# Twelve more chunks per layer as pairs of half products, in one stage ahead of the attention

## The chip, the cores and the metric

The kernel runs on one core of a Trainium2 chip. The metric is the time of one execution on the device in microseconds (us), as the median of several runs. The engines that matter here are PE (matrix products), DVE (vector operations), ACT (scalar engine, activations and copies), POOL (a fourth engine, here mostly an issuer of transfers) and SP (which only issues transfers). Each engine takes its instructions in a fixed order and waits at one until what it needs is there; everything behind it on that engine waits too.

## The reference, cut to what matters

Two layers are applied to 640 tokens (512 of a prompt, 128 of samples). In each, one wide projection `x @ w_in` is cut into parts that feed a gated MLP branch (A), a recurrent branch (B), a latent attention (C), an attention over a memory (M) and the gates that merge them:

```python
(a_u, a_v, a_g, b_x, b_g, c_q, c_kv, c_kr, c_g, m_q, gate_logits) = split_cols(x @ w_in)
oa, v_rows = gmlp_branch(a_u, a_v, ...)       # gelu(a_u) * (mix of layer_norm(gelu(a_v)))
oa = oa * silu(a_g)
ob = rglru_branch(b_x, ...) * silu(b_g)
oc = mla_branch(c_q, c_kv, c_kr, ...) * silu(c_g)
om = mem_attend(m_q, mem_k, mem_v)
g = sigmoid(gate_logits)                       # four gates of 1024 channels
merged = g[:, :, 0] * (oa @ w_a) + g[:, :, 1] * (ob @ w_b) + g[:, :, 2] * (oc @ w_c) + g[:, :, 3] * (om @ w_m)
x = layer_norm(ALPHA * x + merged @ w_out)
```

The change concerns how the parts `a_u` (512 channels, gelu), `c_g` and `b_g` (512 channels each, silu) are computed.

## The kernel before

All matrix products are done in fp32 by parts: each operand is split into a high and a low part (`split`: ACT casts the high part, DVE subtracts it to get the low one), and three products are added: high by high, low by high, high by low.

**Chunks.** A chunk is 128 channels of the projection. `fm_chunk` loads its 1024 x 128 weights (`wraw`, one transfer of 512 KB on SP's queue into one of three `raw` buffers), splits them (`whl`, into one of two `wh` and two `wl` buffers) and issues 48 matmuls of 128 x 320 into an accumulator of two PSUM banks: 8 blocks of the inner dimension, 3 parts, 2 halves of the tokens. An evacuation with gelu or silu follows (`gelu_u`, `silu_into`).

**Pairs of half products.** `fm_pair` computes two chunks at once by a scheme in the manner of Strassen: seven products of half the inner dimension, of 12 matmuls each, in place of eight. It needs four sums of quarters of the operand x (`xt` 1 to 4, made by `x_sums`, written to DRAM as `xsum` and read back by `x_sums_back`), and sums of the weights of the two chunks (`wsum`, on DVE). DVE then adds the products from PSUM (`psum`). Before the change only the merge gates are done so: 14 pairs per layer (the other four chunks of the gates go through `fm_chunk`).

**Order within a layer.** The latent projections c, the projection v (120 matmuls, then gelu on ACT), the latent transposes (`cqT_ps` and others), in layer 0 the memory's keys and values (`mem_kv`), the layer norm of v on DVE, two gelu chunks, the query product `q_ps`, the other gelu chunks, the token mixing (`mix`, which needs the weights `wmx` by way of POOL), the rest of the queries, four silu chunks of C each followed by one quarter of `x_sums`, keys and values, then the attention, into whose gaps a scheduler puts the remaining chunks, and the merge: pairs of gate chunks (`fp`) alternating with the branch products (`y`, 48 matmuls per pair of channels chunks, 24 in the last branch), then the output projection.

Instructions are put on each engine in an order that the scheduler of the framework works out; buffers and PSUM banks are reused in turn. A tile is waited for as a whole: two banks of one accumulator tile count as one thing in this.

Of the kernel before, what the change touches and what calls it, by code (L numbers as in the profile page):

```python
# [19 lines left out]
T = NP_ + NS  # L20
# [16 lines left out]
PRE_U = 2  # L37
# [3 lines left out]
def encoder_step(  # L41
# [141 lines left out]
    xsum = dr.tile([4, 128, 4, 2, TH], F32, name="xsum")  # L183

    for l in range(L):
# [105 lines left out]
        def x_sums(k, xh=xh, xl=xl):  # L291
            x0, x1 = tmp([128, T], "x0"), tmp([128, T], "x1")
            for i, x_ in enumerate((x0, x1)):
                DVE.tensor_tensor(
                    out=x_, in0=xh[i][:, k, :].bitcast(F32), in1=xl[i][:, k, :].bitcast(F32), op=ALU.add
                )
            t12 = tmp([128, T], "t12")
            t1, t2 = t12[:, lo_], t12[:, hi_]
            DVE.tensor_tensor(out=t1, in0=x0[:, lo_], in1=x0[:, hi_], op=ALU.subtract)
            DVE.tensor_tensor(out=t2, in0=t1, in1=x1[:, hi_], op=ALU.add)  # L300
            DVE.tensor_tensor(out=x0[:, hi_], in0=x0[:, hi_], in1=x1[:, hi_], op=ALU.subtract)
            DVE.tensor_tensor(out=x1[:, lo_], in0=x1[:, lo_], in1=t2, op=ALU.subtract)
# [12 lines left out]

        def fm_pair(c, take):
# [8 lines left out]
            ab, cd = acc("fp"), acc("fp")  # L325
            ba, bb, bc, bd = (o[:, j, 0:TH] for o in (ab, cd) for j in range(2))
# [16 lines left out]
            p1, u = t_[:, lo_], t_[:, hi_]  # L343
            wsum(ws[:, b_], r0[:, a_], r1[:, a_])
            wsum(r1[:, a_], r1[:, a_], r1[:, b_])
            wsum(ws[:, a_], r0[:, a_], r1[:, a_])
# [10 lines left out]
            wsum(r0[:, b_], r0[:, b_], ws[:, a_])  # L357
            w1 = whl(r1)
            product(ba, w1, 0, 1, True, False)
# [6 lines left out]
            psum(z0[:, hi_], ba, u, ALU.add)  # L366
            take(0, slice(0, T), z0)
            return z0, z1

# [872 lines left out]
```

## Time and profile before

| what | value |
|---|---|
| median of 3 runs | 1425.04 us (1424.37 to 1427.62) |
| profiled execution: its own time | 1428.68 us |
| its span, first to last instruction | 1427.0 us |
| PE busy | 1391.2 us, 97% of the span |
| DVE busy | 963.4 us, 68% |
| ACT busy | 596.9 us, 42% |
| POOL busy | 119.6 us, 8% |
| mean granted TensorE clock | 0.993 of full speed |

Busy time counts the instructions that compute; PE's matmuls overlap and are counted as one stretch. The profiled execution took 3.64 us more than the median.

### The profile page before, as it was taken

The page shows a single profiled execution, that of the slowest core. Times are in us where ns is not written, and L with a number is a line of the kernel's source. Part 1 is how long each engine was busy: PE and PEld are TensorE (multiplying, and loading weights), DVE is VectorE, ACT ScalarE, POOL GpSimd, SP SyncE. Part 2 cuts the span into 40 slices and gives each one's busy share as a digit, 9 for nine tenths or more (in the row PEclk, how much of TensorE's full clock was granted, in tenths as well). Part 3 has the DMA queues.
Part 4 walks back from the last instruction along what each step waited for, and adds up shares of the span by engine and source line. Part 5 has one row for each costly group of instructions (what it writes and reads, how often), then busy time and mean ns, then how long its engine had stood idle before and what let it go on. Part 6 is the DMA issues. An engine that isn't in the chain of part 4 may idle for free.

```text
span 1427.0 us, 22738 instructions
## 1 busy us (share of the span) xinstructions
PE 1391.2 (97%) x9040; PEld 1281.2 (90%) x9040; DVE 963.4 (68%) x1684; ACT 596.9 (42%) x1019; POOL 119.6 (8%) x248
## 2 busy tenths in 40 slices
PE   8999999999989999999999999999999999999997
PEld 8899987879989999998898999878799899999986
DVE  5664768566577777786844748585766577877866
ACT  5533444355534343444234335353655343334430
POOL 2011110012110000000111102001111000000000
PEclk9999999999999999999999999999999999999999
DMA  7443521523253333227353325126132423322343
GB/s 252 142 137 104 170 82 48 184 91 122 77 165 95 92 93 99 74 89 228 131 181 101 117 92 200 41 73 217 33 126 87 159 95 96 93 84 75 103 156 111
DMA packets 57529, 168.23 MB, mean 118 GB/s; under 512 B 6608, under 2 KB 15728, under 8 KB 55376
## 3 DMA queue, kind: packets, MB, share of 16 engines
q1 hardware_dynamic: 48880, 127.54, 28.7%
q0 software_dynamic: 8544, 39.25, 7.6%
q8 instruction: 71, 1.16, 0.3%
q14 instruction: 34, 0.28, 0.1%
HBM read 140.63 MB, written 24.82 MB: 116 GB/s over the span
## 4 chain that ended last, share of the span: by engine, by line
PE 82%; DVE 9%; DMA 4%; issue 2%; ACT 2%; POOL 0%; DVEq 0%; SPq 0%; ACTq 0%; POOLq 0%
PE fm L122 21%; PE fp L334 19%; PE y L122 12%; PE y_ps L1087 8%; PE v L137 4%; PE c L137 3%; PE sc_ps L693 3%; DMA raw<-in_w_fm 2%; PE pv_ps L717 2%; PE mem L137 2%; DVE wl L148 1%; PE pt_ps L710 1%; PE q_ps L122 1%; DMA mcache<-in_mem_kv 1%; DVE z L340 1%
## 5 line engine op out<-in xcount | busy, mean ns | idle before, releaser
L147 ACT CAST wh<-raw 128x1024 fp32r<-128x1024 f32 (+3 forms) x203 | 191.5, 943 | 367.4 <-PE fp L334 159.3
L148 DVE TENSOR_TENSOR wl<-raw,wh 128x1024 fp32r<-128x1024 f32 (+3 forms) x203 | 222.5, 1097 | 143.1 <-issue 56.1
L122 PE MATMUL fm<-xl,wh 128*128 128x320 f32 x832 | 200.9, 316 | 0.0
L122 PE MATMUL fm<-xh,wh 128*128 128x320 f32 x832 | 200.4, 317 | 0.4 <-DVE oc L527 0.4
L334 PE MATMUL fp<-xt,wh 128*128 128x320 f32 x896 | 149.9, 310 | 6.5 <-ACT wh L147 3.9
L122 PE MATMUL y<-bhl,wh 128*128 128x320 f32 x896 | 147.4, 316 | 2.3 <-DVE macc L969 1.0
L122 PEld LDWEIGHTS fm<-xh,wh 128*128 128x128 f32 x832 | 139.5, 188 | 7.5 <-issue 4.5
L122 PEld LDWEIGHTS fm<-xl,wh 128*128 128x128 f32 x832 | 140.3, 188 | 5.7 <-issue 5.2
L334 PEld LDWEIGHTS fp<-xt,wh 128*128 128x128 f32 x896 | 135.4, 188 | 8.7 <-ACT wh L147 5.5
L122 PE MATMUL fm<-xh,wl 128*128 128x320 f32 x832 | 142.8, 316 | 0.0
L122 PEld LDWEIGHTS y<-bhl,wh 128*128 128x128 f32 x896 | 137.6, 192 | 4.1 <-ACT wh L147 2.1
L122 PEld LDWEIGHTS fm<-xh,wl 128*128 128x128 f32 x832 | 125.8, 189 | 4.4 <-issue 3.3
L334 PE MATMUL fp<-xh,wh 128*128 128x320 f32 x336 | 100.4, 310 | 4.2 <-DVE z L340 2.1
L334 PE MATMUL fp<-xl,wh 128*128 128x320 f32 x336 | 100.4, 310 | 0.0
L334 PE MATMUL fp<-xt,wl 128*128 128x320 f32 x448 | 83.2, 309 | 0.0
L122 PE MATMUL y<-bhl,wl 128*128 128x320 f32 x448 | 76.3, 310 | 0.0
L334 PEld LDWEIGHTS fp<-xt,wl 128*128 128x128 f32 x448 | 70.1, 188 | 0.0
L122 PEld LDWEIGHTS y<-bhl,wl 128*128 128x128 f32 x448 | 68.6, 189 | 0.0
L334 PEld LDWEIGHTS fp<-xh,wh 128*128 128x128 f32 x336 | 63.3, 188 | 4.7 <-issue 4.7
L334 PE MATMUL fp<-xh,wl 128*128 128x320 f32 x336 | 64.0, 313 | 0.0
L334 PEld LDWEIGHTS fp<-xl,wh 128*128 128x128 f32 x336 | 63.4, 189 | 0.0
L340 DVE TENSOR_TENSOR z<-fp,tu 128x320 f32<-128x320 f32 x84 | 40.9, 486 | 31.8 <-PE fp L334 31.7
(326 smaller groups left out, 2317.8 us busy)
## 6 DMA issues: line engine op xcount, KB each, us to landing
raw<-in_w_fm SPq DMA_DIRECT2D x108, 512.0 KB, 3.7
xsum<-xs POOLq DMA_DIRECT2D x32, 320.0 KB, 2.9
xt<-xsum POOLq DMA_DIRECT2D x8, 1280.0 KB, 6.2
raw<-in_w_br SPq DMA_DIRECT2D x20, 512.0 KB, 3.9
mcache<-in_mem_kv SPq DMA_DIRECT2D x8, 1024.0 KB, 5.1
raw<-in_w_out SPq DMA_DIRECT2D x16, 512.0 KB, 4.5
osrc<-oscr POOLq DMA_DIRECT2D x20, 320.0 KB, 3.8
raw<-in_w_v SPq DMA_DIRECT2D x8, 512.0 KB, 3.8
```

The lines of the kernel that those rows point to most:

```text
L122: PE.matmul(out=out[:, j, 0:TH], lhsT=a(k), rhs=b(k)[:, j * TH:(j + 1) * TH], start=(n == 0), stop=(n == len(steps) - 1),)
L137: PE.matmul(out=o[:, 0:width], lhsT=a(ci * nk_per + j)[:, t * 128:(t + 1) * 128], rhs=w[:, j * width:(j + 1) * width], start=(ci == 0 and ...
L147: ACT.copy(out=dst_h, in_=src)
L148: DVE.tensor_tensor(out=dst_l, in0=src, in1=dst_h.bitcast(F32), op=ALU.subtract)
L334: PE.matmul(out=o, lhsT=a[:, k0:k0 + 128], rhs=b[:, k, :], start=(first and n == 0), stop=(n == len(steps) - 1), skip_group_check=True,)
L340: DVE.tensor_tensor(out=out, in0=x, in1=y, op=op)
L693: PE.matmul(out=s[:, 0:nk], lhsT=qT[0:kr_, h, ts_], rhs=kT[h // 4][0:kr_, h % 4, 0:nk], start=True, stop=True,)
L710: PE.transpose(tps[:, k * 128:(k + 1) * 128], p[:, k * 128:(k + 1) * 128], ident)
L717: mm = PE.matmul(out=ops[64 * e:64 * e + 64, hp * 128:(hp + 1) * 128], lhsT=vc[:, k, h * 64:(h + 1) * 64], rhs=pt[:, k * 128:(k + 1) * 128 ...
L1087: PE.matmul(out=o[j], lhsT=mg[k // 2][:, a, k % 2, t * 128:(t + 1) * 128], rhs=wo[k, w][:, j * 512:(j + 1) * 512], start=(k == 0 and p == ...
```

## The change

Twelve chunks per layer (four of `a_u`, four of `c_g`, four of `b_g`) go from `fm_chunk` to `fm_pair`: six more pairs per layer. They stand in one stage right behind the projection v, ahead of the latent transposes. The two gelu pairs and the four silu pairs write their results to DRAM (`gscr`), and `gate_back` reads them back where they are needed (`oa`, `oc`, `ob`). `x_sums` is done ahead of the stage in two halves, keeps its sums in SBUF for it and also writes them to DRAM for the merge. `mem_kv` and the layer norm of v now stand ahead of the six pairs. `fm_pair` itself uses three PSUM banks in place of four: its products with `x11`, `xt2`, `xt1` and `x22` accumulate one upon the other in the bank `ba`, and ACT copies the intermediate states out (`p1`, `u`, and the first state of `bc` into `z1`), so that DVE has three additions from PSUM per pair, not six. The core of the diff:

```diff
+        def x_sums(xh=xh, xl=xl):
...
+            t_ = [new(i) for i in (1, 2, 3, 4)]
+            for k in (0, 2):
...
+                for o, d in zip(t_, (t1, t2, t3, t4)):
+                    split(o[:, 0, ks, :], o[:, 1, ks, :], d)
+            for i, o in enumerate(t_):
+                nc.gpsimd.dma_start(out=xsum[i], in_=o.bitcast(F32))
...
-            ab, cd = acc("fp"), acc("fp")
-            ba, bb, bc, bd = (o[:, j, 0:TH] for o in (ab, cd) for j in range(2))
+            ab, bc = acc("fp"), bank_s("fp_c")[:, 0:TH]
+            ba, bb = (ab[:, j, 0:TH] for j in range(2))
...
+            w1 = whl(r0)
+            product(ba, w1, 0, 11, True, False)
+            ACT.copy(out=p1, in_=ba)
...
             w23 = whl(ws)
-            product(bb, w23, 0, 2, True, True)
-            product(bc, w23, 1, 3, True, False)
-            w1 = whl(r0)
-            product(ba, w1, 0, 11, True, True)
-            ACT.copy(out=p1, in_=ba)
-            psum(u, p1, bb, ALU.subtract)
-            product(bd, w1, 1, 21, True, True)
-            psum(z0[:, lo_], p1, bd, ALU.add)
-            psum(z1[:, hi_], bc, u, ALU.subtract)
+            product(bc, w23, 0, 3, True, False)
+            ACT.copy(out=z1[:, hi_], in_=bc)
+            product(ba, w23, 1, 2, False, False)
+            ACT.copy(out=u, in_=ba)
+            product(bb, w1, 1, 21, True, True)
+            psum(z0[:, lo_], p1, bb, ALU.add)
...
             w1 = whl(r1)
-            product(ba, w1, 0, 1, True, False)
+            product(ba, w1, 0, 1, False, False)
             psum(z1[:, hi_], z1[:, hi_], ba, ALU.subtract)
             product(bc, w1, 1, 4, False, True)
             psum(z1[:, lo_], bc, u, ALU.subtract)
             take(1, slice(0, T), z1)
             w4 = whl(r0[:, b_], 512)
             product(ba, w4, 0, 22, False, True)
-            psum(z0[:, hi_], ba, u, ALU.add)
-            take(0, slice(0, T), z0)
+            take(0, lo_, z0[:, lo_])
+            take(0, hi_, ba)
...
+        x_sums()
+        if l == 0:
+            mem_kv()
...
+        for t in range(NT):
+            layer_norm(v[:, t, :], v[:, t, :], mvv[:, t, 0:1], rv[:, t:t + 1], vlg, vlb)
...
+        for c in (0, 2):
+            gelu_pair(c)
+        for c in (0, 2):
+            silu_pair(1, c, FM_CG)
+        for c in (0, 2):
+            silu_pair(2, c, FM_BG)
```

Within the new stage DVE goes through a pair in this order: the low part of the third weights (changed r1), the addition `z0`, the low part of the last weights, the first weight sum of the next pair, and only then the subtraction `z1` that the last product waits for; in a silu pair three instructions of the silu, the last of them on the last product, stand ahead of the next pair's remaining weight sums. The next pair's r1 is loaded into the buffer that the low part of the third weights has just read.

Three places show how the order on the engines changes.

The first is PE within one pair. Before, in a merge pair (`xt0` to `xt3` are the sums that the code calls xt 1 to 4, `fp_5073` and `fp_5074` the two accumulator tiles; rows between those shown hold the rest of a product):

```order
L334 MATMUL fp_5073<-xt1_3950,wh_5081 128x320 x8
L334 MATMUL fp_5073<-xt1_3950,wl_5082 128x320 x4
L334 MATMUL fp_5074<-xt2_3952,wh_5081 128x320 x8
L334 MATMUL fp_5074<-xt2_3952,wl_5082 128x320 x4
...
L334 MATMUL fp_5073<-xh0_0_100,wl_5110 128x320 x4
...
L334 MATMUL fp_5074<-xh0_1_101,wl_5110 128x320 x4
L334 MATMUL fp_5073<-xt0_3948,wh_5142 128x320 x8
L334 MATMUL fp_5073<-xt0_3948,wl_5143 128x320 x4
L334 MATMUL fp_5074<-xt3_3954,wh_5142 128x320 x8
L334 MATMUL fp_5074<-xt3_3954,wl_5143 128x320 x4
...
L334 MATMUL fp_5073<-xh0_1_101,wl_5173 128x320 x4
```
After, in a pair of the new stage (`fp_1041` holds the banks `ba` and `bb`, `fp_c_1042` is `bc`; `wh_1046` is the high part of the first weights r0, `wh_1066` of their sums, `wh_1110` of the changed r1):

```order
L359 MATMUL fp_1041<-xh0_0_103,wl_1047 128x320 x4
L359 MATMUL fp_c_1042<-xt3_499,wh_1066 128x320 x8
L359 MATMUL fp_1041<-xt2_498,wh_1066 128x320
L359 MATMUL fp_c_1042<-xt3_499,wl_1067 128x320 x4
L359 MATMUL fp_1041<-xt2_498,wh_1066 128x320 x7
L359 MATMUL fp_1041<-xt2_498,wl_1067 128x320 x4
L359 MATMUL fp_c_1042<-xt4_500,wh_1110 128x320 x3
...
L359 MATMUL fp_1041<-xh0_1_104,wl_1047 128x320 x4
L359 MATMUL fp_c_1042<-xt4_500,wh_1110 128x320 x5
L359 MATMUL fp_1041<-xt1_497,wh_1110 128x320 x8
L359 MATMUL fp_1041<-xt1_497,wl_1111 128x320 x4
```
The first weights' product comes first, and the product of `wh_1110` with `xt4` begins (three of its matmuls) ahead of the second product of the first weights.

The second place is DVE at the start of layer 1's stage. Before, the layer norm of v (`v_7216`) is followed by the sums of x for later use:

```order
L161 SCALAR_TENSOR_TENSOR v_7216<-v_7216,mvv_7364,vlg_7212 128x512 x3
L158 RECIPROCAL rv_7365<-rv_7365 128x5
L148 TENSOR_TENSOR wl_7603<-raw_7600,wh_7602 128x512
L162 SCALAR_TENSOR_TENSOR v_7216<-v_7216,rv_7365,vlb_7213 128x512 x5
L294 TENSOR_TENSOR x0_7936<-xh1_0_6528,xl1_0_6530 128x640
```
After, the layer norm (`v_7249`) stands between the work of the first pair: `wl_7597` is the low part of its third weights, `z0_7529` its first addition from PSUM, `ws_7651` a sum of the next pair's weights, `cql_8297` belongs to the latent transposes:

```order
L160 SCALAR_TENSOR_TENSOR v_7249<-v_7249,mvv_7397,vlg_7490 128x512
L496 BN_AGGR mvv_7397<-bnst_7506 128x2
L160 SCALAR_TENSOR_TENSOR v_7249<-v_7249,mvv_7397,vlg_7490 128x512 x4
L157 RECIPROCAL rv_7398<-rv_7398 128x5
L147 TENSOR_TENSOR wl_7597<-raw_7524,wh_7596 128x1024
L161 SCALAR_TENSOR_TENSOR v_7249<-v_7249,rv_7398,vlb_7491 128x512 x5
L365 TENSOR_TENSOR z0_7529<-tu_7531,fp_7527 128x320
L365 TENSOR_TENSOR z1_7530<-fp_c_7528,tu_7531 128x320
L147 TENSOR_TENSOR wl_7627<-raw_7522,wh_7626 128x512
L348 TENSOR_TENSOR ws_7651<-raw_7647,raw_7649 128x512
L150 SCALAR_TENSOR_TENSOR cql_8297<-cqT_ps_8301,vec_6986,cqh_8296 128x512
L365 TENSOR_TENSOR z1_7530<-z1_7530,fp_7527 128x320
```
Ten layer norm instructions now stand ahead of the first pair's addition `z0`.

The third place is SP's queue of loads where the mixing weights `wmx` are fetched in layer 0. Before:

```order
L104 DMA raw_814<-in_w_fm 128x1024
L104 DMA raw_886<-in_w_fm 128x1024
L104 DMA raw_988<-in_w_uqn 128x1024
L104 DMA raw_1055<-in_w_fm 128x1024
L542 DMA wmx_942<-in_w_mix 128x1024
L543 DMA wmx_942<-in_rows 128x512
L535 DMA qT_775<-oc_661 16x640 x16
```
After (`raw_2498` and `raw_2557` are chunks that are computed during the attention, `raw_1578` and `raw_1661` the weights of the remaining queries, keys and values):

```order
L103 DMA raw_1578<-in_w_uqn 128x1024
L103 DMA raw_1661<-in_w_ukv 128x1024
L103 DMA raw_2498<-in_w_fm 128x1024
L103 DMA raw_2557<-in_w_fm 128x1024
L584 DMA wmx_1532<-in_w_mix 128x1024
L585 DMA wmx_1532<-in_rows 128x512
L578 DMA qT_1474<-rp_1481 16x640 x16
```
`wmx` and the transfers of `qT` now stand behind two loads of chunks of a later stage.

## Rows read from the trace of the kernel before

**Rows 1.** The profile page, part 1 and chain of waits by line

```profile
PE 1391.2 (97%) x9040; PEld 1281.2 (90%) x9040; DVE 963.4 (68%) x1684; ACT 596.9 (42%) x1019; POOL 119.6 (8%) x248
...
PE fm L122 21%; PE fp L334 19%; PE y L122 12%; PE y_ps L1087 8%; PE v L137 4%; PE c L137 3%; PE sc_ps L693 3%; DMA raw<-in_w_fm 2%; PE pv_ps L717 2%; PE mem L137 2%; DVE wl L148 1%; PE pt_ps L710 1%; PE q_ps L122 1%; DMA mcache<-in_mem_kv 1%; DVE z L340 1%
```

**Rows 2.** Windows, merge of layer 0: length, then busy time of each engine

```profile
451.00:567.00 116.00, 116.00 (x792) 115.88 (x791) 85.39 (x119) 42.50 (x53) 2.69 (x5) 1.00 0.32 97
```

**Rows 3.** Timeline of PE, layer 0 after v: start, length, instruction

```profile
70.31 0.46 PE L122 MATMUL fm<-xh,wh 128*128 128x320 f32 x2
...
85.45 0.45 PE L122 MATMUL q_ps<-cqh,wh 128*128 128x320 f32 x2
...
89.11 0.54 PE L122 MATMUL fm<-xh,wh 128*128 128x320 f32 x2
...
93.87 2.51 PE L122 MATMUL fm<-xh,wl 128*128 128x320 f32 x16
...
100.91 2.51 PE L122 MATMUL fm<-xh,wl 128*128 128x320 f32 x16
```

**Rows 4.** Timeline of PE, merge of layer 0, last two branches

```profile
567.62 1.33 PE L334 MATMUL fp<-xt,wh 128*128 128x320 f32 x8
...
576.42 1.33 PE L334 MATMUL fp<-xt,wh 128*128 128x320 f32 x8
...
579.94 2.51 PE L122 MATMUL y<-bhl,wh 128*128 128x320 f32 x16
...
586.98 1.33 PE L334 MATMUL fp<-xt,wh 128*128 128x320 f32 x8
...
620.91 2.02 PE L334 MATMUL fp<-xt,wh 128*128 128x320 f32 x12 [1.61 <-ACT wh L147]
...
653.24 0.86 PE L1087 MATMUL y_ps<-wo,mg 128*128 128x512 f32 x3
```

**Rows 5.** Timeline of ACT at the same place

```profile
577.79 1.05 ACT L147 CAST wh<-raw 128x1024 fp32r<-128x1024 f32 x1 [2.85 <-PE fp L334]
```

**Rows 6.** Lines of ACT by form: count, busy time and mean ns

```profile
L147 ACT CAST wh<-raw 128x1024 fp32r<-128x1024 f32 x148 | 155.5, 1051 | 312.6 <-PE fp L334 124.8 <-PE fm L122 79.9 <-PE y L122 43.5
...
L352 ACT COPY tu<-fp 128x320 f32<-128x320 f32 x28 | 11.9, 424 | 31.6 <-PE fp L334 31.6
...
L147 ACT CAST xh<-xraw 128x640 fp32r<-128x640 f32 x8 | 5.5, 727 | 3.1 <-DMA xraw<-in_xT 3.1
```

**Rows 7.** Lines of DVE by form, columns as before

```profile
L148 DVE TENSOR_TENSOR wl<-raw,wh 128x1024 fp32r<-128x1024 f32 x148 | 182.8, 1237 | 124.6 <-issue 56.1 <-PE v L137 22.3 <-ACT wh L147 19.5
L340 DVE TENSOR_TENSOR z<-fp,tu 128x320 f32<-128x320 f32 x84 | 40.9, 486 | 31.8 <-PE fp L334 31.7
...
L323 DVE TENSOR_TENSOR ws<-raw 128x512 f32<-128x512 f32 x56 | 38.6, 690 | 5.1 <-DMA raw<-in_w_fm 4.1
...
L161 DVE SCALAR_TENSOR_TENSOR v<-v,mvv,vlg 128x512 f32<-128x512 f32 x10 | 7.2, 734 | 0.0
```

**Rows 8.** The profile page, DMA issues: count, KB each, us to landing

```profile
raw<-in_w_fm SPq DMA_DIRECT2D x108, 512.0 KB, 3.7
```

**Rows 9.** Tile wmx: its POOL instruction (ns min/median/max) and its transfers

```profile
L545 POOL TENSOR_SCALAR_AFFINE_SELECT wmx<-wmx x2: 1097/1397/1697, 92.1 to 799.3; 128x1024 f32<-128x1024 f32 x2
...
DMA to landing us min/median/max: 4.7/4.7/4.8
```

**Rows 10.** Timeline of ACT, layer 0, behind the projection v

```profile
57.42 2.56 ACT L443 ACTIVATE v<-v 128x512 f32<-128x512 f32 x5
```

**Rows 11.** Timeline of PE, layer 1, first instruction behind the projection v

```profile
775.73 1.03 PE L463 MATMUL cqT_ps<-ident,cb 128*128 128x128 f32 x8
```

**Rows 12.** Windows at the start of the merge; PEclk is last but two

```profile
400.00:404.00 4.00, 3.33 (x13) 2.96 (x13) 2.61 (x7) 1.78 (x2) 1.61 (x3) 0.50 0.77 270
404.00:408.00 4.00, 4.00 (x24) 4.00 (x24) 2.41 (x9) 0.00 (x0) 0.00 (x0) 0.79 0.96 378
```

**Rows 13.** Timeline of PE just ahead of that; in brackets the idle time before

```profile
398.24 0.39 PE L334 MATMUL fp<-xh,wh 128*128 128x320 f32 x1 [2.10 <-DVE vec L821]
```

More of the change, by code (lines that the diff above doesn't have):

```diff
@@ L181, in spill, with gate_back @@
         nc.gpsimd.dma_start(out=oscr[bi][k], in_=src)
-    xsum = dr.tile([4, 128, 4, 2, TH], F32, name="xsum")
+    xsum = dr.tile([4, 128, 2, 4, TH], F32, name="xsum")
+    gscr = [dr.tile([4, 128, T], F32, name=f"gscr{i}") for i in range(3)]
+    def gate_back(i, name):
+        t_ = otile([128, 4, T], F32, name)
+        nc.gpsimd.dma_start(out=t_, in_=gscr[i].rearrange("k p t -> p k t"))
+        return t_
     for l in range(L):
@@ L365, in fm_pair, with silu_pair, gelu_pair @@
             product(ba, w4, 0, 22, False, True)
-            psum(z0[:, hi_], ba, u, ALU.add)
-            take(0, slice(0, T), z0)
+            take(0, lo_, z0[:, lo_])
+            take(0, hi_, ba)
             return z0, z1
+        def silu_pair(i, c, fm):
+            gs = []
+            z = fm_pair(fm + c, lambda e, cols, v_: gs.append((e, cols, v_)))
+            th = [tmp([128, T], f"th{e}") for e in range(2)]
+            for e, cols, v_ in gs:
+                ACT.activation(out=th[e][:, cols], in_=v_, func=AF.Tanh, scale=0.5)
+                DVE.scalar_tensor_tensor(
+                    out=th[e][:, cols], in0=th[e][:, cols], scalar=1.0, in1=v_, op0=ALU.add, op1=ALU.mult
+                )
+            for e in range(2):
+                nc.gpsimd.dma_start(out=gscr[i][c + e], in_=th[e])
+        def gelu_pair(c):
+            gs = []
+            z = fm_pair(FM_U + c, lambda e, cols, v_: gs.append((e, cols, v_)))
+            for e, cols, v_ in gs:
+                ACT.activation(out=z[e][:, cols], in_=v_, func=AF.Gelu_apprx_tanh)
+            for e in range(2):
+                nc.gpsimd.dma_start(out=gscr[0][c + e], in_=z[e])
         a0, a1 = acc("c01"), acc("c23")
@@ L503, in silu_into @@
             DVE.scalar_tensor_tensor(out=halves(dst), in0=halves(dst), scalar=1.0, in1=o, op0=ALU.add, op1=ALU.mult)
-        def gelu_u(c):
-            ACT.activation(out=halves(oa[:, c, :]), in_=fm_chunk(FM_U + c), func=AF.Gelu_apprx_tanh)
-        for c in range(PRE_U):
-            gelu_u(c)
         qT = atile([128, 8, T], F32, "qT")
@@ L535, in encoder_step @@
                 nc.sync.dma_start(out=qT[r + 16 * n:r + 16 * n + 16, h, :], in_=rp[n][16 * h:16 * h + 16, :])
-        for c in range(PRE_U + 1, 4):
-            gelu_u(c)
+        oa = gate_back(0, "oa")
         wmx = otile([128, 1536], F32, "wmx")
@@ L582, in encoder_step @@
         POOL.memset(qT[32:64, 1::2, :], 0.0)
-        for c in range(4):
-            silu_into(oc[:, c, :], FM_CG + c)
-            x_sums(c)
+        oc = gate_back(1, "oc")
         kT = [kvtile([128, 4, NP_], F32, f"kT{i}") for i in range(2)]
```

83 lines of the change are left out of this document (41 added, 42 removed).

## Prediction

> **What bounds the kernel now.** I read the page first: PE is busy 97% of the span and the chain of waits is PE almost throughout, with the chunk matmuls fm and fp and the branch products y as its largest lines [rows 1]. In the merge PE has no gap at all in 116 us, and DVE is busy for 85.39 of them [rows 2]. So what PE does counts in full as long as it is fed, and the question is whether the new stage and the new pair can feed it. One matmul of 320 columns takes 0.1467 us: a chunk of 48 takes 100.91 - 93.87 = 7.04 us [rows 3], two chunks 14.08, and a pair of 84 takes 579.94 - 567.62 = 12.32 [rows 4].
>
> **What it removes.** Twelve pairs replace 24 chunks: 12 x (14.08 - 12.32) = 21.1 us less matmul work. Everything below is what I expect PE to wait for instead.
>
> **Wait inside a pair.** In the new order of PE three matmuls with the third weights (wh_1110) follow the sums' second product. With two wh buffers, those weights go into the buffer that this product reads. ACT's cast starts about 0.04 us after the last matmul that reads the buffer (576.42 + 1.33 = 577.75, cast at 577.79) [rows 4, 5] and takes 1.05 [rows 6]. Only four matmuls (0.59 us) are left to cover it, which leaves 0.55, and handovers of about 0.1 and the copy u that the next product waits for (0.42 [rows 6] against 0.44 of matmuls) bring it to about 0.72. Bounds: nothing, if PE takes the later product first; 1.46, if the copy u (0.42) and the addition z0 (0.49 [rows 7]) lie bare behind the 0.55. I take 0.72, plus 0.06 where one branch matmul stands in between: 0.78. In the merge this meets the 10 full pairs of each layer, which have no slack now [rows 2]: 20 x 0.78 = 15.6 us. The last branch's four pairs are paced by loads already (from 586.98 to 653.24, 16.56 each, for 15.84 of matmuls, with a wait of 1.61 for a cast [rows 4]), and I leave them as they are.
>
> The trace before has its four products in four banks and no gap [rows 2]. The Trainium skill (Perfetto Trace Analysis, Optimizing Tensor Performance, Matmuls) says that independent matmul groups should rotate through PSUM banks, so that one group's evacuation overlaps the next one's matmuls; this change does the opposite. By that rule the three evacuations of a pair lie bare, by my rows there are other matmuls beside two of them; the rule's outcome is the fourth rival.
>
> **The stage's own loop.** The load of the next pair's r1 waits until DVE has split this pair's. From the end of the cast of r1 I follow a silu pair: DVE's split 1.2 [rows 7]; load 3.7 [rows 8] and 0.3 for its issue; the next pair's first weight sum, 0.65 (0.69 less overlap [rows 7]); subtraction z1, 0.45; last product 1.76 with 0.1 of handover; tanh of half a chunk, 0.6 with handover (nearest row the copy, 0.42 [rows 6]); its multiplication 0.45 (as long as z1); two weight sums 1.3; cast of the sums 1.15 with handover; 20 matmuls until the buffer is free, 2.93 and 0.2; cast 1.05. Together 15.85 us per pair. Behind a gelu pair the tanh and its multiplication fall out of the loop and another split comes in: about 14.5. Pairs 2 and 3 follow gelu pairs, 4 to 6 silu pairs: 2 x 14.5 + 3 x 15.85 = 76.5 against 5 x 14.08 = 70.4 before, **+6** per layer. If the loop were hidden, 5 x (13.04 - 14.08) = -5. The loop's largest pieces are rows themselves, so I take +6.
>
> **The stage's start.** In layer 1 the projection v ends at 775.7 [rows 11]. ACT then needs about 3.1 us for the gelus (2.56 for the five [rows 10], and their start) and 2.7 for the first four casts of the x sums (0.73 each, less overlap [rows 6]): 781.5. DVE splits those four behind the row statistics (until 782.3), makes the second half's six sums (4.5), and splits xt1 and xt3 with one more sum between (2.2): 789.0. The second product needs xt3, so PE stands for some 11 us after the first. Then the ten layer norm instructions, 0.67 each (0.73 less overlap [rows 7]), and the split of r1 stand ahead of addition z0, which ends at about 800.8. The third weights' product waits for z0 (same accumulator tile): 802.6. The z1 subtraction has six other DVE instructions ahead (about 3.5), 806.3, and the last product ends at 808. Before, two chunks and the transposes after v came to 775.7 + 14.1 + 1.4 = 791.2: +17. I take **+15**, since part of the transposes may come later in either.
>
> In layer 0, DVE splits the memory's weights behind statistics and x splits: its products end at about 75 rather than at 70.3 [rows 3]. The second product starts near 78; without layer norm the first pair would end at 89.3; the layer norm and two splits of the transposes (8.1 together) hold back z0 by 3.8 and the rest by 1.5: 94.6 against 70.3 + 14.1 = 84.4, **+10**. Bounds for both: 3 and 5, if DVE's queue is reordered by what is ready earlier than I think and only the x sums are late; nothing cannot be, since PE has no other work ready.
>
> **Behind the stage.** The load of wmx stands on SP's queue behind two loads that wait for raw buffers, until DVE has split the query weights. Say that happens at T + 2.6 after the stage; landing is 4.7 later and POOL needs 1.4 [rows 9], handovers 0.6: the mixing can start at T + 9.3. PE has only the first query product, 89.11 - 85.45 = 3.66 [rows 3], where chunks used to lie. **+5.6** per layer (0 if the buffers come free earlier, 9 if T is later by the transposes).
>
> **Hidden.** The new DRAM traffic is 12 results of 328 KB per layer and their return on POOL's queue, with most of the attention's preparation in between. DVE's work in a pair falls by three additions, 1.4 us.
>
> **Sum.** Against the profiled execution's own 1428.68: layer 0 10 + 6 + 5.6, layer 1 15 + 6 + 5.6, merges 15.6, together +63.8: 1492.5. These are differences against the 14.08 of two chunks, so the 21.1 is in them. The median lies 3.64 below the profiled execution: **1489 us**.
>
> **Rivals.**
> 1. Slower, but less: the start costs only its lower bounds (3 and 5), the loop is hidden (-5), wmx costs 3, the merge 15.6. 1428.7 + 8 - 10 + 6 + 15.6 = 1448, less 3.6: 1445. For it speaks that I took the queue order strictly, and that buffer times are from another stage; against it, that every link is a row.
> 2. Faster: PE is fed throughout, and the wait inside the pair disappears. 1425 - 21.1 = 1404, up to 1412 with one wait for wmx per layer. It decides at 21.1 / 32 = 0.66 us of wait per pair over the 12 new and 20 full merge pairs, with nothing lost at the start; the cast alone leaves 0.55 bare, so this needs PE's order to be other than it stands.
> 3. The clock falls in the gaps. After a gap of 2.1 us [rows 13] the granted clock was 0.50 and 0.79 in two windows of 4 us [rows 12]. That is 0.5 x 4 + 0.21 x 4 = 2.8 us per gap; the change brings some six such gaps per layer, and where half of the price is not hidden by DVE's chain that is 12 x 1.4 = 17 us: 1506. Against it: in a stage paced by DVE and ACT a slower PE is partly free. The Trainium skill (TensorE: Matmul & The Clock Gate, Part 1: The HAM clock gate) says that the throttled clock is the default and activity releases it, and the 0.50 of that window, which is 1.2 of 2.4 GHz, agrees.
> 4. The evacuations lie bare: 1.46 per pair in the merge, 20 x (1.46 - 0.78) = 14 more: 1503. It decides only if ACT and DVE are late with them in every pair; in the merge of before they were not [rows 2].
> 5. No difference: the loop is hidden (-10), the start costs its lower bounds (8), and neither wmx nor the pair in the merge loses anything: -2.
>
> **How the numbers follow.** Likeliest, 0.55: 1489, own range 1462 to 1512. Rival 1: 0.18. Rival 2: 0.08. Rival 3: 0.11. Rival 4: 0.05. Rival 5: 0.03. A measurement of this kernel tells about 0.2% (2.9 us) from no change. Slower 0.89, same 0.03, faster 0.08. The range 1440 to 1516 leaves out rival 2, rival 5 and the ends of the others, some 0.18.
>
> **What would show it.** In the trace of after: PE busy less by about 21 us and a longer span; waits of PE for the cast wh of some 0.5 to 0.8 us in each merge pair, with pairs 20.1 us apart instead of 19.36; six pairs of the stage 14.5 to 15.9 apart; a gap of 10 us after v in layer 1, ended by DVE's xt; a wait at mix for wmx. I am wrong if the merge pairs stay at 19.4 (the third weights are cast early) or if the stage's pairs follow at 12.3 to 13 (the loads run ahead).

## The result and the profile after

The changed kernel takes **1531.0 us** (median of 4 runs, 1526.34 to 1534.55), the kernel before 1425.67 in the same comparison: a ratio of 1.0736 (95% interval 1.0703 to 1.0769). The forecast was 1489 and its range ended at 1516: the sign is right, the size 42 us short. The profiled execution has a span of 1530.3 us at a mean granted clock of 0.971 (before 1427.0 and 0.993).

The page of after, part 1 and the chain of waits by engine; it answers to [rows 1]:

```profile
PE 1419.3 (93%) x8896; PEld 1281.5 (84%) x8896; DVE 990.9 (65%) x1676; ACT 652.0 (43%) x1159; POOL 128.6 (8%) x254
...
PE 71%; DVE 7%; ACT 5%; DMA 5%; issue 2%; POOL 0%; DVEq 0%; SPq 0%; ACTq 0%; POOLq 0%
```

PE has 144 matmuls less and is busy 28.1 us *longer* than before. Its idle time went from 1427.0 - 1391.2 = 35.8 to 1530.3 - 1419.3 = 111.0 us: 75 more, where the forecast of +63.8 with 21.1 us less matmul work meant 85. So the waits come to about what was forecast in all. What was not forecast is that the matmuls themselves count for more: 28.1 + 21.1 = 49 us by the page. Busy time times what the granted clock lacks of 1, added over windows of 2 us, is 33.8 us in after and 7.7 before: 26 of the 49 are the clock. The rest holds matmuls ahead of a wait, whose ends are modelled (0.31 us where one in a row takes 0.147). PE stands still 127 times in after and 49 times before, so these ends make some 78 x 0.16 = 13 us, which are waits and not work; about 10 us stay open.

The waits of PE in after, by what they waited for (us in all, times, longest):

```profile
PE fp_c L359 <- ACT wh L146: 30.9, 37, 2.3
PE fp L359 <- ACT tu L379: 9.2, 9, 2.9
PE fp L359 <- DVE z L365: 7.1, 5, 2.9
PE mix L594 <- POOL wmx L587: 6.5, 2, 3.2
...
PE fp_c L359 <- ACT xt L146: 6.1, 2, 4.8
...
PE mkT_ps L236 <- ACT mkv L233: 5.0, 1, 5.0
PE mem L136 <- DVE wl L147: 5.0, 1, 5.0
```

The first line is the cast of changed weights inside and between pairs; the last four lines are the stage's start and the mixing behind it.

**By place.** The merge of layer 0 begins 35.2 us later than before (last gate matmul at 420.51, before 385.35) and is 17.6 us longer (to `y_ps` at 706.00: 285.5, before 267.9). In layer 1 the same two are +35.1 and +16.6. That is all of the loss: 35.2 + 35.1 + 17.6 + 16.6 = 104.5. Forecast were 21.6, 26.6, 7.8 and 7.8.

**One pair of the merge.** PE in after, merge of layer 0; start, length, instruction, idle time before it; it answers to [rows 4]:

```profile
493.68 1.33 PE L359 MATMUL fp_c<-xt,wh 128*128 128x320 f32 x8
...
496.61 0.75 PE L359 MATMUL fp<-xt,wl 128*128 128x320 f32 x4
497.91 0.71 PE L359 MATMUL fp_c<-xt,wh 128*128 128x320 f32 x3 [0.55 <-ACT wh L146]
498.46 0.30 PE L359 MATMUL fp<-xh,wh 128*128 128x320 f32 x1
...
503.63 0.42 PE L121 MATMUL y<-bhl,wh 128*128 128x320 f32 x1
...
514.29 0.90 PE L359 MATMUL fp_c<-xt,wh 128*128 128x320 f32 x5
```

ACT at the same place, the cast that answers to [rows 5] and the copy `u` behind it:

```profile
496.81 1.05 ACT L146 CAST wh<-raw 128x1024 fp32r<-128x1024 f32 x1 [0.70 <-PE fp L359]
497.76 0.42 ACT L379 COPY tu<-fp 128x320 f32<-128x320 f32 x1
```

The four matmuls of 496.61 would let the next follow at 497.20; it starts at 497.91, 0.71 later, when the cast is through. The copy `u` stands behind the cast on ACT, so `bb`, in the tile that it reads, can't fill the hole: its product starts at 498.46. Smaller handovers follow (0.17 at 503.63 for the next cast), and pairs are 514.29 - 493.68 = 20.61 us apart instead of 19.36. In a window of 116 us of this merge PE is idle for 3.91 us and DVE busy for 70.74, where before there was no gap [rows 2]:

```profile
490.00:606.00 116.00, 112.09 (x741) 108.37 (x740) 70.74 (x91) 44.47 (x66) 2.69 (x5) 1.00 0.28 88
```

**The stage.** PE in after, layer 0: two waits of the start, then the first product of the weight sums from the second pair on, and twice the end of the twenty matmuls that the cast of the third weights waits for (the row of `fp<-xt,wl`):

```profile
70.51 2.08 PE L136 MATMUL mem<-wl,mem_h 128*128 128x512 f32 x4 [4.95 <-DVE wl L147]
...
83.76 0.69 PE L236 MATMUL mkT_ps<-ident,mkv 128*128 128x128 f32 x2 [4.97 <-ACT mkv L233]
...
103.25 1.44 PE L359 MATMUL fp_c<-xt,wh 128*128 128x320 f32 x8 [0.16 <-ACT wh L146]
...
117.47 1.44 PE L359 MATMUL fp_c<-xt,wh 128*128 128x320 f32 x8 [0.39 <-ACT wh L146]
...
120.51 0.75 PE L359 MATMUL fp<-xt,wl 128*128 128x320 f32 x4
...
133.61 1.79 PE L359 MATMUL fp_c<-xt,wh 128*128 128x320 f32 x8 [2.33 <-ACT wh L146]
...
138.18 0.74 PE L359 MATMUL fp<-xt,wl 128*128 128x320 f32 x4
...
151.28 2.30 PE L359 MATMUL fp_c<-xt,wh 128*128 128x320 f32 x8 [2.34 <-ACT wh L146]
...
168.97 2.50 PE L359 MATMUL fp_c<-xt,wh 128*128 128x320 f32 x8 [2.33 <-ACT wh L146]
```

The starts of the sums' products are 14.22, 16.14, 17.67 and 17.69 us apart. Ahead of each pair that follows a silu pair PE waits 2.33, and the eight matmuls behind the wait take 1.79, 2.30 and 2.50 us instead of 1.44. The windows say why (PE busy is the third number, the granted clock the last but two):

```profile
133.00:135.00 2.00, 1.39 (x8) 1.39 (x9) 1.38 (x2) 0.55 (x1) 0.00 (x0) 0.87 0.15 56
135.00:137.00 2.00, 2.00 (x9) 2.00 (x8) 0.00 (x0) 0.17 (x1) 0.00 (x0) 0.50 0.00 0
...
153.00:155.00 2.00, 2.00 (x10) 2.00 (x9) 0.00 (x0) 0.00 (x0) 0.00 (x0) 0.51 0.00 0
```

PE is fully busy in 135 to 137 and gets half the clock, the level of 1.2 GHz, after it stood still from about 131.3 to 133.6. From the end of v to the first `ss_ps` the clock costs 11.3 us in layer 0 and 12.1 in layer 1, counted as above; before it was 0 in both.

DVE in the same pair, which sets the wait:

```profile
144.56 0.69 DVE L348 TENSOR_TENSOR ws<-raw 128x512 f32<-128x512 f32 x1 [1.43 <-DMA raw<-in_w_fm]
...
147.10 1.22 DVE L401 SCALAR_TENSOR_TENSOR th<-th,z 128x640 f32<-128x640 f32 x2
148.28 0.49 DVE L401 SCALAR_TENSOR_TENSOR th<-th,fp 128x320 f32<-128x320 f32 x1
148.68 0.68 DVE L348 TENSOR_TENSOR raw<-raw 128x512 f32<-128x512 f32 x1
149.40 0.69 DVE L348 TENSOR_TENSOR ws<-raw 128x512 f32<-128x512 f32 x1
```

It is the forecast's loop: the first weight sum waits for r1 to land, and the other two stand behind the silu of the last product.

**Layer 1's start and the mixing.** PE in after, from the first instruction behind v (it answers to [rows 11]) to the second pair:

```profile
827.74 1.04 PE L529 MATMUL cqT_ps<-ident,cb 128*128 128x128 f32 x8
...
840.06 0.63 PE L359 MATMUL fp_c<-xt,wh 128*128 128x320 f32 x1 [4.75 <-ACT xt L146]
...
841.51 1.17 PE L359 MATMUL fp_c<-xt,wh 128*128 128x320 f32 x3 [0.82 <-DVE xt L147]
...
855.87 2.50 PE L359 MATMUL fp<-xt,wh 128*128 128x320 f32 x8 [2.86 <-DVE z L365]
...
864.68 1.33 PE L359 MATMUL fp_c<-xt,wh 128*128 128x320 f32 x8
```

and SP's queue in layer 0 just ahead of `wmx`, for which `mix` waits 3.23 us (until 191.22):

```profile
181.36 3.23 SPq L103 DMA_DIRECT2D raw<-in_w_fm  x2
184.70 0.56 SPq L584 DMA_DIRECT2D wmx<-in_w_mix  x1
```

### The profile page after: what moved, and what is told of

Its sections match the earlier page's. It is cut to its first block, busy times and chain, and to the rows that moved or that the text cites. A ratio compares the mean times of both kernels' runs of the same rounds, so it can differ in the third digit from the quotient of the medians.

```text
span 1530.3 us, 22600 instructions
## 1 busy us (share of the span) xinstructions
PE 1419.3 (93%) x8896; PEld 1281.5 (84%) x8896; DVE 990.9 (65%) x1676; ACT 652.0 (43%) x1159; POOL 128.6 (8%) x254
## 4 chain that ended last, share of the span: by engine, by line
PE 71%; DVE 7%; ACT 5%; DMA 5%; issue 2%; POOL 0%; DVEq 0%; SPq 0%; ACTq 0%; POOLq 0%
PE fp L359 17%; PE y L121 12%; PE fm L121 11%; PE fp_c L359 8%; PE y_ps L1124 7%; ACT wh L146 3%; PE sc_ps L732 3%; PE v L136 2%; PE pv_ps L756 1%; DMA raw<-in_w_fm 1%; PE c L136 1%; PE pt_ps L749 1%; DVE wl L147 1%; DMA mcache<-in_mem_kv 1%; PE q_ps L121 1%
## 5 line engine op out<-in xcount | busy, mean ns | idle before, releaser
L359 PE MATMUL fp_c<-xt,wh 128*128 128x320 f32 x640 | 126.2, 331 | 42.0 <-ACT wh L146 30.9
L359 PE MATMUL fp<-xh,wh 128*128 128x320 f32 x480 | 147.6, 319 | 12.8 <-ACT tu L379 9.2
L359 PEld LDWEIGHTS fp_c<-xt,wh 128*128 128x128 f32 x640 | 103.4, 199 | 54.1 <-ACT wh L146 41.8
L121 PE MATMUL fm<-xl,wh 128*128 128x320 f32 x448 | 115.5, 328 | 0.0
L121 PE MATMUL fm<-xh,wh 128*128 128x320 f32 x448 | 110.6, 321 | 0.0
L121 PE MATMUL fm<-xh,wl 128*128 128x320 f32 x448 | 85.4, 326 | 0.0
L121 PEld LDWEIGHTS fm<-xh,wh 128*128 128x128 f32 x448 | 75.7, 190 | 7.3 <-issue 5.6
L121 PEld LDWEIGHTS fm<-xl,wh 128*128 128x128 f32 x448 | 76.4, 189 | 5.6 <-issue 4.6
L348 DVE TENSOR_TENSOR ws<-raw 128x512 f32<-128x512 f32 x80 | 55.1, 689 | 34.4 <-DMA raw<-in_w_fm 33.8
L359 PEld LDWEIGHTS fp<-xh,wl 128*128 128x128 f32 x480 | 76.5, 190 | 0.0
```

What stands on the lines that cost most here:

```text
L121: PE.matmul(out=out[:, j, 0:TH], lhsT=a(k), rhs=b(k)[:, j * TH:(j + 1) * TH], start=(n == 0), stop=(n == len(steps) - 1),)
L348: DVE.tensor_tensor(out=out, in0=x, in1=y, op=ALU.add)
L359: PE.matmul(out=o, lhsT=a[:, k0:k0 + 128], rhs=b[:, k, :], start=(first and n == 0), stop=(n == len(steps) - 1), skip_group_check=True,)
```

## The experiments

**Theory.** Four causes: (1) inside a pair, `bb` in `ba`'s tile leaves the cast of the third weights and the copy `u` bare; (2) the stage starts late, behind the x sums; (3) its loop of one raw buffer and the silu on DVE leaves a gap per pair; (4) the gaps bring the clock down. **Rivals:** the place alone costs the time, whatever the chunks are computed with; or the loop is bound by another chain, and a filled gap gives the clock's share back by itself. Ratios are to the kernel before on the same chip, with their 95% intervals. In e1 and e2 the operand sum `xt2` keeps the sign of the other pair's scheme, so they compute other values with the same instructions.

### Taking the change apart

**e1: the kernel before with the new pair body alone.**

```diff
-            ab, cd = acc("fp"), acc("fp")
-            ba, bb, bc, bd = (o[:, j, 0:TH] for o in (ab, cd) for j in range(2))
+            ab, bc = acc("fp"), bank_s("fp_c")[:, 0:TH]
+            ba, bb = (ab[:, j, 0:TH] for j in range(2))
...
```

> The kernel before with the new body of fm_pair alone, used where it always was, in the merge; no new stage. Theory (the pair itself waits in the merge: pairs 20.6 us apart in the trace of after instead of 19.36, and both merges together 33 us longer): 1425.7 + 33 = 1459 us, pairs of the full branches 20.6 apart. Rival (the merge is longer only because the stage ahead of it left something late): 1426 to 1432, pairs 19.4 apart.

Measured: 1460.28 us, 1.0228 (1.0207 to 1.025). The merges are 285.5 and 283.3 us long, as in after. The pair's form alone costs 33 us, twice the 15.6 forecast.

**e2: the whole change, with the old pair body** (four banks, three more additions on DVE).

```diff
-            ab, bc = acc("fp"), bank_s("fp_c")[:, 0:TH]
-            ba, bb = (ab[:, j, 0:TH] for j in range(2))
+            ab, cd = acc("fp"), acc("fp")
+            ba, bb, bc, bd = (o[:, j, 0:TH] for o in (ab, cd) for j in range(2))
...
```

> The changed kernel with the old body of fm_pair (four banks, six additions on DVE), in the stage and in the merge. Theory (pair and stage are separate costs, 33 and 70): the merges go back to what they were, the stage stays slow through its loads and its start: 1531 - 33 = 1498, give or take 8. Rival (the accumulation in one bank is also what slows the stage): the six pairs of the stage come to 14.1 us apart or less, and the time to 1460 or less.

Measured: 1476.21, 1.0343 (1.032 to 1.0367). The merges are back at 268.7 and 268.9. The stage's pairs are 13.0 to 13.3 us apart, so the rival is partly right: with the old body the pair in the stage also loses most of its waiting, though there are three raw buffers and the silu is on DVE as in after. So cause (3) is a loop of the new body in this place, not of the place alone. Whether the order of its products or their tiles make it is not taken apart; a tile of its own for `bb` (e4) does not end it.

**e3: the twelve chunks as plain chunks, in the same place.**

```diff
-            z = fm_pair(fm + c, lambda e, cols, v_: gs.append((e, cols, v_)))
...
+                v_ = fm_chunk(fm + c + e)
```

> The changed kernel with the twelve chunks in the same stage, same place, same way through DRAM, but by plain chunks and not by pairs; x_sums as in the change; merge as in the change. Theory (the stage is slow because pairs there wait for x sums at the start and for the loop of r1's load): chunks need neither, so only the merges' 33 and what stands behind the stage (two waits for wmx and what follows, some 14) are left: 1425.7 + 33 + 14 = 1473. Rival (the place is the cause: layer norm, transposes and DRAM traffic ahead of the attention cost what is lost): 1500 or more.

Measured: 1486.01, 1.0407 (1.0386 to 1.0428), between the two. Less the merges' 33 it would be 1453: the place costs some 26 us with no pair in it. Not all of this is the place of the x sums: with them ahead of v, and the other mends of e9, it is still 13 (e15).

**e4: `bb` gets a tile of its own.** An accumulator tile has two banks, so `ba` and `bb` lie in different banks in after too; what changes is that they are no longer one thing to wait for.

```diff
-            ba, bb = (ab[:, j, 0:TH] for j in range(2))
+            ba, bb = ab[:, 0, 0:TH], bank_s("fp_b")[:, 0:TH]
```

> The changed kernel with the product bb in a tile of its own, not in the tile of ba, so that it need not wait for ACT's copy of ba and the order on PE puts it behind the sums' second product, over the cast of r1. Theory (the wait in the pair is that cast, uncovered since bb shares ba's tile): merge pairs back to 19.4 to 19.6, 20 x 1.2 = 24 us, and a few us in the stage: 1500 to 1507. Rival (the accumulation in one bank is the cause, whatever the order): pairs stay at 20 or more, 1520 or more.

Measured: 1492.53, 1.046 (1.0439 to 1.0481): better than expected. PE in e4, a pair of the merge:

```profile
484.53 1.34 PE L359 MATMUL fp_c<-xt,wh 128*128 128x320 f32 x8
...
487.47 0.75 PE L359 MATMUL fp<-xt,wl 128*128 128x320 f32 x4
488.05 0.31 PE L359 MATMUL fp_b<-xh,wh 128*128 128x320 f32 x1
...
503.89 1.34 PE L359 MATMUL fp_c<-xt,wh 128*128 128x320 f32 x8
```

`bb`'s product follows without a gap and covers the cast; pairs are 503.89 - 484.53 = 19.36 us apart, as before. Cause (1) is shown, from both sides (e1 and e4). In the stage the pairs are still 15.6 to 17.1 us apart in layer 0 where they follow silu pairs.

### The stage's loop and the clock

**e5: a fourth raw buffer** (room from one buffer of the weight sums), so that r1 is loaded a pair earlier.

```diff
-            ws = wtile("ws", 1024, "ws")
+            ws = wtile("ws", 1024, "ws", 1)
...
```

> The changed kernel with four raw buffers in place of three (one buffer of the weight sums given up for it, the final layer norm's rows kept elsewhere). Theory of the prediction (the load of r1 into the one buffer that comes round is a link of the stage's loop): the load runs a pair ahead, silu pairs come to 14.9 us apart or less instead of 16.1 to 17.7, about 8 us per layer, 1515. Rival (the loop runs through PE, ACT's tanh, DVE's silu and the next weight sums, and the load is beside it): silu pairs stay at 16 to 17.7, 1526 to 1533.

Measured: 1512.79, 1.0623 (1.0591 to 1.0655). From the second pair on they are 13.54 to 13.57 us apart.

**e6: twelve matmuls whose result is not used, ahead of the sums' products of the silu pairs.** They only keep PE at work.

```diff
+            if fill:
+                sp_ = bank_o("fill")[:, 0:TH]
+                for n in range(fill):
+                    PE.matmul(
+                        out=sp_, lhsT=w1[0][:, 0:128], rhs=xt[11][0][:, 0, :],
...
```

> The changed kernel with 12 matmuls of no use (1.76 us at full clock) ahead of the second product of every pair but the gelu ones of the stage, where PE stands 2.3 us in silu pairs; their result is not read. Theory (the clock that falls in the stage costs time: some 11 us per layer of slower matmuls, of which those on the loop count): the granted clock in the stage rises to 0.97 or more, silu pairs come to about 16 us apart, 4 pairs x 1.2 x 2 = 10 us less: 1521. Rival (a slower PE is free in a stage paced by ACT and DVE): 1531 or up to 5 more.

Measured: 1525.07, 1.072 (1.0682 to 1.0757). PE in e6:

```profile
149.69 1.92 PE L375 MATMUL fill<-xh,wh 128*128 128x320 f32 x12
152.20 1.45 PE L359 MATMUL fp_c<-xt,wh 128*128 128x320 f32 x8 [0.58 <-ACT wh L146]
```

The matmuls behind the gap run at full speed and the pairs are 16.16 us apart, not 17.67: the loop itself is the 15.85 forecast plus a handover, and the last 1.5 us are the clock. But the whole kernel gains 2 us by the ratios and 6 by the medians, which their intervals do not tell from nothing: the pair behind the second gelu pair, which had little to wait for, also got the twelve matmuls and is now 15.4 us behind it, from 14.22. By the windows the clock cost 8 us in after from the second pair's sums to the end of the sixth, both layers together, and costs nothing there in e6; the time from v to `mix` fell by 1.5 us per layer. So in this loop the clock's fall is an addition to DVE's chain, but this filling does not win it back for the kernel.

**e7: the next pair's weight sums stand ahead of the last product in the code**, so that DVE has them ahead of the silu.

```diff
+            if mid:
+                mid()
             product(ba, w4, 0, 22, False, True)
```

> The changed kernel with the next pair's loads and weight sums issued ahead of a pair's last product, so that they stand ahead of its silu on DVE. Theory (the loop passes from the last product through tanh and silu to the next weight sums): silu pairs fall to the 14.2 to 14.6 us of the gelu ones, 7 intervals x 2.5 = 18 us less: 1513. Rival (the load or the clock paces the stage): silu pairs stay above 15.5, 1523 to 1533.

Measured: 1513.77, 1.0644 (1.0606 to 1.0682); pairs 14.2 to 15.1 us apart. Either link of the loop, broken alone, gives some 13 to 16 us: cause (3).

### The start

**e8: the x sums stand ahead of the projection v.**

```diff
+        x_sums()
         v = otile([128, NT, 512], F32, "v")
...
-        x_sums()
         if l == 0:
             mem_kv()
```

> The changed kernel with x_sums ahead of the projection v. Theory (the stage's start waits for the x sums: directly in layer 1, 8 to 9 us, and in layer 0 through the split of the memory's weights behind them on DVE, 5 us): 1531 - 13 = 1518, and less by some more if the clock does not fall there. Rival (the layer norm and the copies behind it hold the first pair anyway): 1528 to 1532, the first pair ends where it did.

Measured: 1503.56, 1.056 (1.0524 to 1.0596), 15 us better than expected. In layer 0 the first pair's sums are multiplied at 73.61 (in after at 84.80), and the waits at `mem` and `mkT_ps` are gone but for 0.46 us. Cause (2) costs 25 us, of which the forecast had only a part.

### Mends together

**e9: the edits of e4, e5 and e8 together.**

> The changed kernel with bb in its own bank, four raw buffers and x_sums ahead of v: three mends together. Theory (three separate costs, which add): 1.0736 - 0.0276 - 0.0113 - 0.0176 = 1.017 of the kernel before, about 1450. Rival (they share their gaps, so that one uncovers another): 1.025 or more, 1461 and up.

Measured: 1429.4, 1.0039 (1.002 to 1.0059). The three alone gain 0.0276 + 0.0113 + 0.0176 = 0.0565 of the time before, together 0.0697: 99 us where 81 add up, with some 12 us either way by the intervals. Where the surplus comes from is not shown. It is not the clock: by the windows that now costs 3.1 and 3.7 us in the stages, for 11.3 and 12.1, and e5 and e8 alone already take 9 and 15 us of these 23 away, more than the 17 of e9. PE still waits for `wmx` (1.83 and 3.6) and in the first pairs for a low part behind the layer norm (5.8 in all).

**e10: `wmx` by POOL's queue.**

```diff
-        nc.sync.dma_start(out=wmx[:, 0:1024], in_=ins["w_mix"][l])
+        nc.gpsimd.dma_start(out=wmx[:, 0:1024], in_=ins["w_mix"][l])
...
```

> The same with the mixing weights wmx loaded by POOL's queue, so that they don't stand behind two loads of a later stage on SP's. Theory (mix waits for wmx behind those loads, 3 us per layer and a slower clock behind it): 6 us less than the three mends alone. Rival (POOL's queue is no earlier, since it holds the return of the gelu results, or the x sums' buffers come free no earlier): within 3 us of it.

Measured: 1438.8, 1.0086 (1.0057 to 1.0115), 7 us worse than e9. On POOL's queue `wmx` stands behind the stage's results and is issued at 155.5, on SP's it was 151.9. PE in e10:

```profile
161.34 0.79 PE L639 MATMUL k_ps<-ckh,wl 128*128 128x512 f32 x1 [4.70 <-DVE wl L147]
```

The wait moved to the keys and grew: DVE splits their weights no later than in e9 (from 160.08, there from 160.63), but there the products of `mix` stood ahead of them on PE and covered it.

**e11: as e10, the layer norm of v behind all pairs.**

```diff
-        for t in range(NT):
-            layer_norm(v[:, t, :], v[:, t, :], mvv[:, t, 0:1], rv[:, t:t + 1], vlg, vlb)
...
             silu_pair(2, c, FM_BG)
 
...
+        for t in range(NT):
+            layer_norm(v[:, t, :], v[:, t, :], mvv[:, t, 0:1], rv[:, t:t + 1], vlg, vlb)
```

> The same with the layer norm of v moved behind the six pairs as well. Theory (ten layer norm instructions hold the first pair's additions): 3 to 6 us per layer less than with wmx alone, so 6 to 12. Rival (layer norm then stands ahead of the rope products and of mix on DVE and gives it all back there): within 3 us, or more.

Measured: 1442.05, 1.0121 (1.009 to 1.0152). The six pairs are 12.32 us apart from the first on, but `mix` starts at 168.95 in layer 0, later than in e10 (164.01). The ten layer norm instructions now stand on DVE (149.87 to 157.7) ahead of the low part of the remaining queries' operand, `cql`, for which PE waits 7.92 us at `q_ps`. What the pairs gained is lost there; the intervals of e10 and e11 overlap.

**e12: as e11, with the old pair body** (the edit of e2, with the sign of the sums as they are made here: `psum(u, p1, bb, ALU.add)`).

> The same as the one with wmx and layer norm late, but with the old pair of four banks in place of the new one with bb in its own bank (with the sign of one operand sum adapted). Theory (what cost time in the new pair was bb's tile alone, so that both forms now feed PE alike): within 6 us of it. Rival (the new order, with the first weights' product ahead and three additions fewer on DVE, is better, or worse, by itself): 8 us or more apart.

Measured: 1436.92, 1.0087 (1.0056 to 1.0119), within the expected 6 us of e11. Once `bb` has its own tile, the two bodies are worth about the same.

**e13: as e9, the load of `wmx` right behind the pairs in the code**, so that it goes out ahead of the chunks' loads.

```diff
             silu_pair(2, c, FM_BG)
 
+        wmx = otile([128, 1536], F32, "wmx")
...
+        nc.sync.dma_start(out=wmx[:, 0:1024], in_=ins["w_mix"][l])
```

> The kernel of e9 with the load of wmx ahead of the past keys' loads on SP's queue, before the loads of chunks that it waited behind. In e9 PE waited 5.4 us for wmx at mix (1.83 in layer 0, 3.6 in layer 1), and 5.8 us in the first pairs for a late low part of weights. Theory (the wait for wmx is a queue position and nothing else): 4 to 6 us less than e9, 1424 us. Rival (the wait only moves, as it did when wmx went to POOL's queue): within 2 us of e9, or above, with a new wait at k_ps or v_ps.

Measured: 1421.66, 0.9977 (0.9964 to 0.999), 9 us below e9 by the ratios. The wait for `wmx` (5.4 us in e9) is gone, but in its place `mix` waits 5.8 us for DVE's `mixb` between its parts. The profiled executions are only 2.7 us apart (1423.3 and 1420.6; that of e9 was its fastest of ten), so how much of the 9 this wait was worth is not shown.

**e14: as e13, the layer norm between the gelu pairs and the silu pairs.**

```diff
         for c in (0, 2):
             gelu_pair(c)
+        vlg, vlb = tmp([128, 512], "vlg"), tmp([128, 512], "vlb")
...
         for c in (0, 2):
             silu_pair(1, c, FM_CG)
```

> As e13, and the layer norm of v stands behind the two gelu pairs, not ahead of the first. Theory: the first pairs' wait for the low part of the third weights (1.98 and 3.87 us in e9, behind the layer norm on DVE) goes, 4 to 6 us less than e13: about 1419, below the kernel before. Rival (DVE has no slack in the silu pairs either): the wait comes back in the later pairs or at mix, within 2 us of e13.

Measured: **1412.76 us, 0.9907 (0.989 to 0.9925)**: faster than the kernel before by 13 us, and 10 us below e13 by the ratios where 4 to 6 were expected; the waits of 5.8 us in the first pairs are gone, and where the rest comes from was not followed. The page of e14, part 1, and PE in its stage:

```profile
PE 1368.5 (97%) x8896; PEld 1254.7 (89%) x8896; DVE 984.3 (70%) x1676; ACT 646.5 (46%) x1159; POOL 131.7 (9%) x254
```

```profile
121.76 1.34 PE L359 MATMUL fp_c<-xt,wh 128*128 128x320 f32 x8
...
134.08 1.34 PE L359 MATMUL fp_c<-xt,wh 128*128 128x320 f32 x8
```

The pairs are 12.32 us apart, their matmul time, and the clock is 1.00 from the end of v to `ss_ps` in both layers. PE is busy 1391.2 - 1368.5 = 22.7 us less than before and idle 1408.6 - 1368.5 = 40.1, about as before (35.8).

**e15: as e9, with plain chunks in the stage.**

> The kernel of e9 with the twelve chunks of the stage as plain chunks (fm_chunk) in the same place; the merge keeps the new pair with its own bank for bb, the x sums stay ahead of v. It tells where the 21.1 us of saved matmuls are. Theory (fed pairs keep their saving, and the place costs what e9 lacks): 1450 us, 21 above e9, the stage 21 / 2 longer per layer than in e9. Rival (the pairs of the stage lose their saving again to waits, the place costs little): within 8 us of e9, 1422 to 1437.

Measured: 1438.17, 1.0095 (1.0077 to 1.0112), 8 us above e9: between theory (21) and rival (0). With the layer norm and `wmx` where e9 has them, the pairs keep 8 of the 21.1 us; the place costs chunks 13 us.

## Why the prediction was wrong in size

**Direction: right, for its reasons.** PE is not fed, and each wait that the forecast named is there. Its sum of idle time was right to 10 us (85 against 75, or 88 with the modelled ends); that PE's busy time would fall by 21 us was wrong.

**The wait inside a pair: mechanism right, size wrong.** The term "0.78 per pair" measured 1.25 (20.61 - 19.36), and 34 us in both merges for 15.6. Of the 0.72 taken for cast and copy, 0.71 came true; the 0.54 that was left out are waits of 0.1 to 0.2 each behind it, at `z0` and at the casts of the next weights, for which nothing stands ready either. Seven pairs in a row of layer 0, two changes of branch among them, take 145.1 us (472.67 to 617.77) where they took 135.8 (431.86 to 567.62): 1.33 more each, so some 13 of that merge's 17.6 us for its ten full pairs. The rest lies at the merge's start and in the last branch, which the forecast left as it was: its pairs are 17.0 to 17.9 us apart for 16.56. Rival 4 (1.46 per pair) was nearer in size; but the additions of DVE that it laid bare are mostly covered; it is ACT's cast, which `bb` could cover if it had not to wait for the copy `u`. The rule from the Trainium skill (Perfetto Trace Analysis, Optimizing Tensor Performance, Matmuls), that independent matmul groups should rotate through PSUM banks, is not what e4 tests: `bb` had another bank than `ba` before it, and a tile of its own alone gives the merge's 33 us back.

**The stage's own loop: right, up to the clock.** 14.5 was 14.22; 15.85 was 16.14 in the first silu pair and 16.16 in e6. The rest of the 17.7 is the clock's.

**The start: layer 1 near, layer 0 not.** In layer 1 the second product was through its waits 13.8 us after v where 13.3 was forecast (841.51 - 827.74), but the first pair ended at v + 37 for v + 32.3. In layer 0 the memory ended at 77 for 75, but then came a link that I had not looked for: the copies of `mkv` stand on ACT behind a cast of weight sums, which waits for DVE, which waits for a load. The transposes `mkT_ps` wait 4.97 us for them, and the first pair ended at 102.9, not 94.6. The forecast had this link at nothing.

**Behind the stage: right.** `mix` waited 3.2 us for `wmx` per layer, with the product of keys in between; forecast were 5.6 with nothing there.

**The steps that failed: the merge pair's wait, and the clock.** Two terms of the sum were too small, and neither alone makes up the 42 us. The first is the wait inside a pair above: 18.6 us over both merges (34.2 - 15.6), shown by e1 and e4.

The second is the clock, which was a rival and not a term. I made "the clock falls in the gaps" (17 us) an alternative to my sum. It comes with it: the same gaps that the sum counts bring it about. It was 23.4 us in the stages. The trace agrees with the rule cited there (the Trainium skill, TensorE: Matmul & The Clock Gate, Part 1: The HAM clock gate): behind the gaps the granted clock is 0.50, the level of 1.2 GHz. The argument against it, that in a stage paced by DVE a slower PE is partly free, is wrong in this loop: the buffer for the third weights is free when PE has read the sums' weights. The twenty matmuls that read them took 4.57 us (133.61 to 138.18) instead of 3.04 (117.47 to 120.51), and the pairs are further apart by the same 1.53 (17.67 for 16.14).

The loss ahead of the merges is 35.2 + 35.1 - 21.6 - 26.6 = 22 us above the forecast. Some 13 of it lie between v and the end of the first pair (102.9 for 94.6 and v + 37 for v + 32.3), where the clock costs 11 by the windows and layer 0 has its link of copies; 4 lie in the five pairs behind it, where the clock costs 8; 5 lie behind the stage, where it costs 5. So most of the 22 can be the clock's, but an experiment shows it for the paced pairs alone (e6); how the clock and the late copies share the start is open. With the 18.6 of the merges, 1489 + 22 + 18.6 = 1530.

**The faster rival was not absurd.** Its 1404 to 1412 needed PE fed throughout, which this change is not; e14 is, with five mends, and takes 1412.8. How the 8 us that e14 lacks of the 21.1 are divided among x sums, layer norm and DRAM was not tried.

## What to carry to other kernels

Before products are put into fewer banks, ask of each evacuation what PE can do meanwhile *without the same tile*: here a tile of its own for one product was worth 33 us, at the same arithmetic. Where a stage is forecast to have gaps on PE, price the clock's fall as part of each gap, not as another case. And the mends of this starved stage were worth more together than one by one, so one that gains little alone isn't refuted; but a load moved to another queue only takes a new place in a line, and what counts is what stands ahead of it there.

## What was not expected of the hardware

Behind waits of 2.33 us the granted clock was 0.50, in a stretch in which PE was busy for 50.84 of 60 us. It did not fall behind each of them: of the six such waits in after, the last of layer 1 has its eight matmuls at full speed.

```profile
930.60 1.43 PE L359 MATMUL fp_c<-xt,wh 128*128 128x320 f32 x8 [2.34 <-ACT wh L146]
```

With the pairs 13.54 apart (e5) and with the wait cut to 0.58 by other matmuls (e6), the clock in the same window of layer 0 is 1.00. The windows of after, e5 and e6, one row of each:

```profile
116.00:176.00 60.00, 50.84 (x297) 47.54 (x296) 32.82 (x47) 23.24 (x37) 3.78 (x7) 0.91 0.31 101
```

```profile
116.00:176.00 60.00, 57.91 (x379) 55.14 (x379) 42.37 (x64) 28.76 (x48) 7.05 (x13) 1.00 0.46 145
```

```profile
116.00:176.00 60.00, 56.57 (x367) 53.18 (x366) 35.67 (x53) 25.08 (x41) 4.32 (x8) 1.00 0.32 106
```
